# A hand-ordered end of the mixers in a hybrid decoder layer

## The chip, the core and the metric

The kernel runs on one core of a Trainium2 chip. The metric is the device time of one execution in microseconds: 386.02 us is the median of three runs (385.05 to 387.39). TensorE does matmuls, VectorE (DVE) and ScalarE (ACT) elementwise work, GpSimd (POOL) some of it too, and SyncE (SP) issues most DMAs. Each engine runs its own instruction stream in a fixed order; semaphores tie the streams together.

## The reference, cut to what matters

One decoder layer over 256 prompt positions and 8 x 4 decode positions, 288 columns together, model width 1024. The part in which the change lies, in short:

```python
def rmsnorm(x, g):
    y = x * rsqrt(mean(x * x, axis=-1) + 1e-6)
    return y * g

proj = rmsnorm(x) @ w_in                       # -> q | k | v | gate_b | gate_c | u
attn = dilated_attention(rope(q), rope(k), v)  # prompt by itself, decode against its cache
gated_in = gate_c * u
conv = conv_w[0] * u_pad[:, 0:T] + conv_w[1] * u_pad[:, 1:T+1] + conv_w[2] * u_pad[:, 2:T+2]
conv_out = gate_b * conv
mixed = concat(rmsnorm(attn, g_att), rmsnorm(conv_out, g_conv)) @ w_out
x = x + rmsnorm(mixed, n_att_post)
x = x + rmsnorm(square(relu(rmsnorm(x) @ w_up)) @ w_down)
```

## The kernel before

All activations stand transposed: 128 partitions hold features, the 288 columns are positions. Each weight matrix is cut into sub-blocks of 128 x 1024 (s = 0 to 95), which hold the eight 128x128 pieces that yield one chunk of 128 output features; two sub-blocks make one block of 1 MB, and SyncE fetches the blocks in order into three buffers (`raw`). A block's buffer is free for the third block behind it once both its sub-blocks have been split.

A product of 32-bit numbers is made of three matmuls (`mm3`): a weight or an activation is split into a high part, which is a cast by ScalarE, and a low part, which is the difference, taken by VectorE (`split_w`). Then high x high, high x low and low x high are summed in PSUM. So one row (128 input features of one chunk) is three matmuls of 288 columns, and a chunk of eight rows is 24. High and low parts of weights go to buffers of two pools: `splp` (three pairs) and, late in the mixers, `spx` (two pairs).

Sub-blocks 0 to 23 are the input projection. Of them 18 and 20 give the conv gate C of channels 2 and 3 (a channel here is 128 conv features), 19 and 21 give u, and 22 and 23 give the output gate: chunks `B2` and `B3`. Sub-blocks 24 to 31 are the output projection: chunks `mix0` to `mix7`. The first four rows of such a chunk read the normed attention (`mh[0]`, `ml[0]`), the last four the normed conv (`mh[1]`, `ml[1]`). 32 to 63 are the up projection and 64 to 95 the down projection.

At the end of the mixers these steps stand between the products:

- the filter of a channel: one scaling by ScalarE and two taps by VectorE (tile `cv`), then the product with the gate (`conv_out`: a scaling of the PSUM tile to `bs`, and three products into `co`, of 256, 28 and 4 columns);
- the selection of the decode attention: a mask by VectorE (`om`), four small matmuls (`dsel`, the picks, put between rows of B2), and a copy into `aT`;
- the norm of the 32 decode columns (`attd`): a square, a sum over chunks of features, a matmul with a constant matrix that sums over partitions (`ss_attd`), the inverse root by logarithm, exponential and a Newton step (`rsqrt_rows`), the scaling, high and low parts;
- the same for the conv half over all 288 columns (`ss_conv`, `mh1`, `ml1`).

Five projection chunks (`NW = 5`) have their attention half done first, chunk by chunk, while the conv norm is under way; then each of them has its conv half (`mix_half(m, 1, False)`), directly followed by `post` (ScalarE squares the chunk and scales it, VectorE sums the squares). Chunks 5 to 7 are whole products.

The order on each engine is a scheduler's, steered by `tc.high_priority()` and `after(...)` (nothing inside is issued ahead of the named instruction). GpSimd takes the low parts of sub-blocks 24 and 25 (`POOL_LO`) and that of conv chunk 1 (`POOL_ML`). The high and low parts of 25 to 28 are made in four quarters.

Of the kernel before, what the change touches and what calls it, by code (L numbers as in the profile page):

```python
# [10 lines left out]
F32 = mybir.dt.float32  # L11
F32R = mybir.dt.float32r
# [4 lines left out]
P = 128  # L17
# [16 lines left out]
TAIL = ((0, 1, 5), (1, 0, 0), (0, 0, 1), (0, 0, 2), (1, 0, 1), (0, 0, 3), (1, 0, 3), (1, 1, 5), (0, 0, 4), (1, 0, 4),  # L34
        (0, 1, 7), (0, 0, 6), (1, 0, 6), (1, 0, 7))
ORDER = (0, 1, 2, 3, 5, 4, 6, 7)

POOL_LO = (24, 25)
POOL_ML = (1,)

SQ_POOL = 6

# [68 lines left out]
def layer(ctx, tc, xt, vec, cst, kt, vt, st, wts, o_y, o_k, o_v, o_cs):  # L111
# [38 lines left out]
    nc.gpsimd.memset(m512, 1.0 / 512)  # L150


    def split_w(s, parts=1, pool=splp, eng=None):
        raw = blocks[s // 2][:, (s % 2) * 1024:(s % 2) * 1024 + 1024]
        hi = pool.tile([P, 1024], F32R, tag="hi", name=f"hi{s}")
        lo = pool.tile([P, 1024], F32R, tag="lo", name=f"lo{s}")
        n = 1024 // parts
        for i in range(parts):
            cs = slice(i * n, (i + 1) * n)
            a = nc.scalar.copy(hi[:, cs], raw[:, cs])  # L160
            b = (eng or nc.vector).tensor_sub(lo[:, cs], raw[:, cs], hi[:, cs].bitcast(F32))  # L161
# [334 lines left out]
    def d_select(g):  # L496
        om = sm.tile([P, AW], F32, tag="ds", name=f"om{g}", bufs=1)
        nc.vector.scalar_tensor_tensor(
            om.rearrange("p (h d) -> p h d", h=H), dpv[g].rearrange("p (h d) -> p h d", h=H), dpt[g][1],
            c[:, C_DG:C_DG + H].unsqueeze(2).to_broadcast([P, H, HD]), ALU.mult, ALU.mult)  # L500
        ps = pa.tile([P, 512], F32, tag="a", name=f"dsel{g}")

        def pick(p):
            nc.tensor.matmul(ps[:, p * 16:(p + 1) * 16], lhsT=om[:, p * P:(p + 1) * P],
                             rhs=c[:, C_SEL:C_SEL + 16], start=True, stop=True)
            if p == 3:
                nc.vector.tensor_copy(aT[:, :, SEQ + 16 * g:SEQ + 16 * g + 16],
                                      ps[:, 0:64].rearrange("p (c t) -> p c t", c=4))

        return [lambda p=p: pick(p) for p in range(4)]  # L510
# [61 lines left out]
    def group_norm(src, vcol, c0, c1, hf, ssq, nm, pool, tag):  # L572
        n = c1 - c0
        if mh[hf] is None:
            mh[hf] = act.tile([P, 4, NT], F32R, tag="act", name=f"mh{hf}")
            ml[hf] = act.tile([P, 4, NT], F32R, tag="act", name=f"ml{hf}")
        dh, dl = mh[hf], ml[hf]
        s = nrm.tile([P, NT], F32, tag="s", name=f"s_{nm}")
        if n <= 64:
            for ch in range(4):  # L580
                nc.scalar.mul(src[:, ch, c0:c1], src[:, ch, c0:c1], vv[:, vcol + ch:vcol + ch + 1])
        chain = rsqrt_rows(ssq, m512, n, s[:, :n], nm, pool, tag)
        if n <= 64:
            nc.vector.tensor_mul(src[:, :, c0:c1], src[:, :, c0:c1], s[:, :n].unsqueeze(1).to_broadcast([P, 4, n]))
            nc.scalar.copy(dh[:, :, c0:c1], src[:, :, c0:c1])  # L585
            d = nc.vector.tensor_sub(dl[:, :, c0:c1], src[:, :, c0:c1], dh[:, :, c0:c1].bitcast(F32))
            return chain[0], d.ins
        for ch in range(4):
            nc.vector.scalar_tensor_tensor(src[:, ch, c0:c1], src[:, ch, c0:c1], vv[:, vcol + ch:vcol + ch + 1],
                                           s[:, :n], ALU.mult, ALU.mult)  # L590
            nc.scalar.copy(dh[:, ch, c0:c1], src[:, ch, c0:c1])
            e = nc.gpsimd if hf == 1 and ch in POOL_ML else nc.vector
            e.tensor_sub(dl[:, ch, c0:c1], src[:, ch, c0:c1], dh[:, ch, c0:c1].bitcast(F32))
# [53 lines left out]
    es.close()
    pt = ctx.enter_context(tc.tile_pool(name="pt", bufs=6, space=PSUM))
    spx = ctx.enter_context(tc.tile_pool(name="spx", bufs=2, side="right"))
    sqd = cv.tile([P, 4, ND], F32, tag="w", bufs=4, name="sqd")  # L650
    acc_d = cv.tile([P, ND], F32, name="acc_d")
# [7 lines left out]
    b3 = conv_b(3, 23)  # L659
    sq3 = cv.tile([P, NT], F32, tag="w", bufs=4, name="sqc3")  # L660
    with tc.high_priority():
        conv_out(*b3)
        nc.scalar.square(sq3, co[:, 3])
        with after(last_mm[0]):
            group_norm(co, V_CONV, 0, NT, 1, [acc_c, sq3], "conv", pt, "o")
    NW = 5
    ws = [take(24, 0)]
    with after(*chain[:1]):
        ws += [take(25, 0)] + [split_w(26 + m, parts=4, pool=spx) for m in range(2)] + [take(28, 0)]
# [228 lines left out]
```

## Time and profile before

| | |
|---|---|
| median of three runs | 386.02 us (385.05 to 387.39) |
| the profiled execution | 386.36 us, of it 384.6 us span |
| busy in the span | PE 365.8 us (95%), DVE 235.3 (61%), ACT 193.8 (50%), POOL 42.0 (11%) |
| TensorE's granted clock, mean | 0.987 of full speed |
| read from HBM | 73.40 MB, 197 GB/s over the span |
| chain that ended last | PE 79%, DVE 10%, DMA 3%, ACT 3%, issue 2% |

The span is the time from the first to the last instruction; what lies around it counts in the device time too. A share of busy time is a mean over stages with different limits, so a change in one stage is read from the timeline of that stage. In a timeline a row gives the start, the duration and, in brackets, how long the engine stood idle before it and what ended that. Rows of matmuls overlap: a matmul of 288 columns is shown with some 0.30 us, while the next starts 0.13 after it. A fp32 matmul is shown as two instructions. L197 to L199 are the three matmuls of `mm3`.

### The profile page before, as it was taken

What the parts mean: (1) busy time and instruction counts of PE and PEld (TensorE: products, weight loads), DVE (VectorE), ACT (ScalarE), POOL (GpSimd) and SP (SyncE); (2) the same over time, 40 slices, a digit from 0 to 9 for tenths busy, and PEclk for the clock granted to TensorE, in tenths of its full rate; (3) what the DMA queues carried; (4) which work ended last, traced back from release to release, by engine and by line L of the source; (5) the groups of instructions that cost most, each with busy time, mean ns of one, the idle gap of its engine ahead of it and who ended that gap; (6) DMA issues with size and microseconds to landing.
All of it is one profiled execution on the core that took longest, in us unless ns stands there. A gap on an engine that the chain in (4) does not pass through costs nothing.

```text
span 384.6 us, 6800 instructions
## 1 busy us (share of the span) xinstructions
PE 365.8 (95%) x2728; PEld 338.1 (88%) x2728; DVE 235.3 (61%) x424; ACT 193.8 (50%) x370; POOL 42.0 (11%) x69
## 2 busy tenths in 40 slices
PE   7899999999999799999999999999999999999971
PEld 7799777676885699989999999999999999999960
DVE  4998637456484876599886666666434344434416
ACT  5779445534452648537675555555444344434310
POOL 5414100114412500000000000000000000000012
PEclk9999999999999899999999999999999999999996
DMA  6995599996991353801553535353535353542003
GB/s 204 385 402 227 165 416 422 404 356 239 403 418 49 107 201 119 319 3 33 193 211 120 210 114 216 116 211 120 211 118 211 119 210 119 210 125 95 2 0 123
DMA packets 18575, 76.23 MB, mean 198 GB/s; under 512 B 2032, under 2 KB 9200, under 8 KB 11632
## 3 DMA queue, kind: packets, MB, share of 16 engines
q1 hardware_dynamic: 17680, 74.59, 52.5%
q10 hardware_dynamic: 864, 1.22, 0.8%
q8 instruction: 21, 0.34, 0.4%
q14 instruction: 10, 0.08, 0.1%
HBM read 73.40 MB, written 2.40 MB: 197 GB/s over the span
## 4 chain that ended last, share of the span: by engine, by line
PE 79%; DVE 10%; DMA 3%; ACT 3%; issue 2%; SPq 1%; POOL 1%; DVEq 0%; ACTq 0%; POOLq 0%
PE dn L197 9%; PE dn L198 9%; PE dn L199 9%; PE up L197 8%; PE up L199 7%; PE up L198 7%; DMA raw<-wts 3%; PE mix L197 2%; PE mix L198 2%; PE dpv L493 2%; PE mix L199 2%; PE qk L199 2%; PE qk L197 2%; PE qk L198 2%; PE d L449 2%
## 5 line engine op out<-in xcount | busy, mean ns | idle before, releaser
L161 DVE TENSOR_TENSOR lo<-raw,hi 128x1024 fp32r<-128x1024 f32 (+1 forms) x104 | 114.8, 1115 | 81.9 <-ACT hi L160 81.7
L160 ACT CAST hi<-raw 128x1024 fp32r<-128x1024 f32 (+1 forms) x109 | 99.6, 930 | 105.1 <-PE dn L198 56.7
L197 PE MATMUL dn<-fh,hi 128*128 128x288 f32 x256 | 75.8, 296 | 0.0
L198 PE MATMUL dn<-fl,hi 128*128 128x288 f32 x256 | 75.6, 295 | 0.0
L199 PE MATMUL dn<-fh,lo 128*128 128x288 f32 x256 | 75.4, 295 | 0.0
L198 PE MATMUL up<-hl,hi 128*128 128x288 f32 x248 | 73.5, 297 | 0.0
L197 PE MATMUL up<-hh,hi 128*128 128x288 f32 x248 | 73.1, 296 | 0.0
L199 PE MATMUL up<-hh,lo 128*128 128x288 f32 x248 | 73.0, 294 | 0.0
L199 PEld LDWEIGHTS dn<-fh,lo 128*128 128x128 f32 x256 | 48.3, 189 | 0.0
L198 PEld LDWEIGHTS dn<-fl,hi 128*128 128x128 f32 x256 | 48.1, 188 | 0.0
L197 PEld LDWEIGHTS dn<-fh,hi 128*128 128x128 f32 x256 | 48.0, 188 | 0.0
L199 PEld LDWEIGHTS up<-hh,lo 128*128 128x128 f32 x248 | 46.8, 189 | 0.1
L198 PEld LDWEIGHTS up<-hl,hi 128*128 128x128 f32 x248 | 46.6, 188 | 0.1
L197 PEld LDWEIGHTS up<-hh,hi 128*128 128x128 f32 x248 | 46.4, 187 | 0.0
L813 POOL TENSOR_TENSOR mg<-mg,y_f 128x288 f32<-128x288 f32 x1 | 1.0, 1009 | 232.2 <-ACT y_f L209 232.2
L774 DVE SCALAR_TENSOR_TENSOR r<-up,s 128x288 f32<-128x288 f32 x32 | 14.1, 455 | 14.1 <-PE up L199 14.1
L199 PE MATMUL qk<-xh,lo 128*128 128x288 f32 x64 | 18.7, 303 | 2.2 <-DVE lo L250 1.9
L197 PE MATMUL mix<-mh,hi 128*128 128x288 f32 x64 | 19.6, 306 | 1.0 <-ACT mh L585 1.0
L197 PE MATMUL qk<-xh,hi 128*128 128x288 f32 x64 | 19.6, 306 | 0.8 <-ACT hi L249 0.8
L198 PE MATMUL mix<-ml,hi 128*128 128x288 f32 x64 | 19.9, 310 | 0.0
L199 PE MATMUL mix<-mh,lo 128*128 128x288 f32 x64 | 19.5, 305 | 0.0
L198 PE MATMUL qk<-xl,hi 128*128 128x288 f32 x64 | 19.1, 299 | 0.0
(238 smaller groups left out, 628.5 us busy)
## 6 DMA issues: line engine op xcount, KB each, us to landing
raw<-wts SPq DMA_DIRECT2D x45, 1024.0 KB, 4.8
k<-kt SPq DMA_DIRECT2D x16, 640.0 KB, 9.2
v<-vt SPq DMA_DIRECT2D x9, 1024.0 KB, 13.0
raw<-wts SPq DMA_DIRECT2D x4, 512.0 KB, 8.1
o_y<-mg SPq DMA_DIRECT2D x8, 144.0 KB, 1.8
v<-vt SPq DMA_DIRECT2D x2, 512.0 KB, 11.4
x<-xt SPq DMA_DIRECT2D x3, 288.0 KB, 4.4
c<-cst SPq DMA_DIRECT2D x1, 838.0 KB, 9.7
```

Of the source, the lines that this page charges most:

```text
L160: a = nc.scalar.copy(hi[:, cs], raw[:, cs])
L161: b = (eng or nc.vector).tensor_sub(lo[:, cs], raw[:, cs], hi[:, cs].bitcast(F32))
L197: nc.tensor.matmul(ps, lhsT=a, rhs=xh, start=start, stop=False)
L198: nc.tensor.matmul(ps, lhsT=a, rhs=xl, start=False, stop=False)
L199: return nc.tensor.matmul(ps, lhsT=lo[:, j * P:(j + 1) * P], rhs=xh, start=False, stop=stop)
L449: nc.tensor.matmul(ps[32 * i:32 * i + 32, 0:n], lhsT=qbd[:, p, 4 * g + i], rhs=t[:, i, 0:n], start=p == 0, stop=p == 3, tile_position=(0, ...
L493: nc.tensor.matmul(dpv[g][32 * i:32 * i + 32], lhsT=pt[:, j, 32 * i:32 * i + 32], rhs=t[i], start=False, stop=j == 4, tile_position=(0, 32 ...
L774: nc.vector.scalar_tensor_tensor(r, ps[:, :NT], 0.0, s2, ALU.max, ALU.mult)
L813: nc.gpsimd.tensor_mul(mg[:, 0], mg[:, 0], y)
```

## The change

The end of the mixers, from the split of sub-block 23 to the last conv row of projection chunk 4, is put into a block in which the orders of TensorE, VectorE and ScalarE are those of the code. GpSimd has no low parts any more. 26 to 28 are split in whole operations (`high_w`, `low_w`; 28's low part in two halves), 25 too. The splits of 23 and 24 and the filters of channels 2 and 3 stand ahead of the selection, and the picks one row later in B2. The decode columns get their gain by one product on VectorE in place of four on ScalarE. The conv half of chunks 0 to 4 runs row by row: row 0 of all five chunks, then row 1, and so on; the `post` operations follow behind all of it. `prompt_norm` does what `group_norm` did for the prompt.

```diff
-POOL_LO = (24, 25)
-POOL_ML = (1,)
...
-            ready[s] = split_w(s, parts=4 if s in (1, 2) or 25 <= s <= 28 else 1, eng=nc.gpsimd if s in POOL_LO else None)
+            ready[s] = split_w(s, parts=4 if s in (1, 2) else 1)
...
-    picks = d_select(1)
-    b2 = conv_b(2, 22, [lambda: [f() for f in picks[0:2]], lambda: [f() for f in picks[2:4]]])
...
-    with tc.high_priority():
-        nc.scalar.square(sqd, aT[:, :, SEQ:NT])
-        d = nc.vector.tensor_reduce(acc_d, sqd.rearrange("p c t -> p t c"), axis=mybir.AxisListType.X, op=ALU.add)
-        chain = group_norm(aT, V_ATT, SEQ, NT, 0, [acc_d], "attd", pt, "o")
-    with after(chain[0], d.ins):
-        conv_out(*b2)
+    ahead(22)
...
+    with tc.manual_schedule(engines={mybir.EngineType.PE, mybir.EngineType.DVE, mybir.EngineType.Activation}):
+        ahead(23)
+        ahead(24)
+        ys = [conv_y(ch) for ch in (2, 3)]
+        picks = d_select(1)
+        b2 = g_in(22, "B2", [lambda: 0, lambda: [f() for f in picks[0:2]], lambda: [f() for f in picks[2:4]]])
...
+        nc.scalar.square(sqd, ad)
+        nc.vector.tensor_reduce(acc_d, sqd.rearrange("p c t -> p t c"), axis=mybir.AxisListType.X, op=ALU.add)
+        nc.vector.tensor_mul(ad, ad, vv[:, V_ATT:V_ATT + 4].unsqueeze(2).to_broadcast([P, 4, ND]))
+        rsqrt_rows([acc_d], m512, ND, s_d, "attd", pt, "o")
+        nc.vector.tensor_mul(ad, ad, s_d.unsqueeze(1).to_broadcast([P, 4, ND]))
+        nc.scalar.copy(mh[0][:, :, SEQ:NT], ad)
+        conv_out(2, b2, ys[0])
+        nc.vector.tensor_sub(ml[0][:, :, SEQ:NT], ad, mh[0][:, :, SEQ:NT].bitcast(F32))
         sq_add(acc_c, co[:, 2], "sqc2", False)
+        ahead(25)
+        b3 = g_in(23, "B3")
+        ws = [take(24, 0), take(25, 0)] + [high_w(26 + i, spx) for i in range(2)]
+        conv_out(3, b3, ys[1])
...
+        ws.append(high_w(28, splp))
+        low_w(26, ws[2])
+        low_w(27, ws[3])
+        low_w(28, ws[4], 0, 512)
...
+        mix_rows(0, 0, range(4))
+        mix_rows(1, 0, range(2))
+        s_c = nrm.tile([P, NT], F32, tag="s", name="s_conv")
+        rsqrt_rows([acc_c, sq3], m512, NT, s_c, "conv", pt, "o")
...
+        conv_norm(0)
+        low_w(28, ws[4], 512)
+        for ch in range(4):
+            nc.vector.tensor_sub(ml[1][:, ch], co[:, ch], mh[1][:, ch].bitcast(F32))
+            if ch < 3:
+                conv_norm(ch + 1)
+        mix_rows(1, 0, range(2, 4))
+        for m in range(2, NW):
+            mix_rows(m, 0, range(4))
+        for j in range(4):
+            for m in range(NW):
+                mix_rows(m, 1, [j])
...
     for m in range(8):
         if m < NW:
-            mix_half(m, 1, False)
             ps = pss[m]
```

VectorE around the selection of the second decode group, before (`uu3` is the last input of the filters, `lo23` the low part of sub-block 23, `cv3` the taps of channel 3, `om1` the mask, `dsel1` what the picks give):

```order
L537 TENSOR_TENSOR uu3_1521<-u3_1496,s0_157 128x288
L546 SCALAR_TENSOR_TENSOR cv3_1636<-gt_685,vv_78,cv3_1636 128x304 x2
L498 SCALAR_TENSOR_TENSOR om1_1554<-dpv1_1525,rd1_1421,c_177 128x512
L161 TENSOR_TENSOR lo23_1562<-raw11_255,hi23_1561 128x1024
L507 COPY aT_182<-dsel1_1556 128x4x16
L654 TENSOR_REDUCE acc_d_1608<-sqd_1607 128x32
L552 TENSOR_TENSOR bs2_1628<-B2_1565,s0_157 128x288
```

And after the change:

```order
L545 TENSOR_TENSOR uu3_1523<-u3_1498,s0_157 128x288
L158 TENSOR_TENSOR lo23_1559<-raw11_255,hi23_1558 128x1024
L158 TENSOR_TENSOR lo24_1563<-raw12_264,hi24_1562 128x1024
L554 SCALAR_TENSOR_TENSOR cv2_1566<-gt_685,vv_78,cv2_1566 128x304 x2
L554 SCALAR_TENSOR_TENSOR cv3_1570<-gt_685,vv_78,cv3_1570 128x304 x2
L506 SCALAR_TENSOR_TENSOR om1_1574<-dpv1_1527,rd1_1421,c_177 128x512
L515 COPY aT_182<-dsel1_1576 128x4x16
L668 TENSOR_REDUCE acc_d_1620<-sqd_1619 128x32
```

The mask stood behind one filter's taps and ahead of `lo23`; now it stands behind `lo23`, `lo24` and the taps of both channels.

ScalarE behind the conv half of the projection, before (`hi29` and `hi30` are the high parts for chunks 5 and 6; `q_m`, `ssm`, `mg` and `gm` are the post operations of the chunk named at the right):

```order
L160 CAST hi29_1908<-raw14_268 128x1024
L699 ACTIVATE ssm_1823<-mix0_1741 128x288
L700 ACTIVATE mg_1820<-mix0_1741,vv_78 128x288
L721 ACTIVATE gm_1824<-mix0_1741,vpp_1826 128x288
L699 ACTIVATE q_m1_1856<-mix1_1754 128x288
L700 ACTIVATE mg_1820<-mix1_1754,vv_78 128x288
L160 CAST hi30_1912<-raw15_270 128x1024
L699 ACTIVATE q_m2_1872<-mix2_1767 128x288
L700 ACTIVATE mg_1820<-mix2_1767,vv_78 128x288
```

And after the change, from the first post operation on (`hi29` stands right ahead of it):

```order
L729 ACTIVATE ssm_1860<-mix0_1693 128x288
L730 ACTIVATE mg_1857<-mix0_1693,vv_78 128x288
L750 ACTIVATE gm_1861<-mix0_1693,vpp_1863 128x288
L729 ACTIVATE q_m1_1869<-mix1_1694 128x288
L730 ACTIVATE mg_1857<-mix1_1694,vv_78 128x288
L729 ACTIVATE q_m2_1873<-mix2_1695 128x288
L730 ACTIVATE mg_1857<-mix2_1695,vv_78 128x288
L729 ACTIVATE q_m3_1877<-mix3_1696 128x288
L730 ACTIVATE mg_1857<-mix3_1696,vv_78 128x288
L729 ACTIVATE q_m4_1881<-mix4_1697 128x288
L730 ACTIVATE mg_1857<-mix4_1697,vv_78 128x288
L157 CAST hi30_1889<-raw15_270 128x1024
```

`hi30` stood behind the post operations of chunks 0 and 1; now it stands behind those of all five chunks.

## Rows read from the trace of the kernel before

**Rows 1.** Stretches of the span: busy us (instructions) by engine, PEclk, DMA share, GB/s.

```profile
132.00:136.00 4.00, 3.99 (x17) 3.77 (x17) 4.00 (x13) 2.78 (x10) 0.58 (x1) 0.57 0.57 188
136.00:160.00 24.00, 24.00 (x181) 23.83 (x179) 16.75 (x28) 16.43 (x33) 0.91 (x1) 1.00 0.55 192
```

**Rows 2.** Timeline of TensorE, 109 to 160 us: start, us, engine, line, operation, tiles.

```profile
109.71 0.65 PE L475 MATMUL dt<-ident,ds 128*128 128x128 f32 x4
...
120.85 0.40 PE L197 MATMUL B<-xh,hi 128*128 128x288 f32 x1
...
122.15 0.52 PE L504 MATMUL dsel<-c,om 128*128 128x16 f32 x4
...
128.43 0.29 PE L199 MATMUL B<-xh,lo 128*128 128x288 f32 x1
...
131.64 0.40 PE L197 MATMUL mix<-mh,hi 128*128 128x288 f32 x1 [1.01 <-ACT mh L585]
...
135.91 0.30 PE L199 MATMUL mix<-mh,lo 128*128 128x288 f32 x1
...
159.64 0.65 PE L205 MATMUL ss_mix<-ssm,m 128*128 128x288 f32 x2
```

**Rows 3.** The chain that ended last, 125 to 132 us: start, us, what.

```profile
126.58 2.28 DVE co L557
...
128.88 0.45 ACT sqc L569
...
129.36 0.46 DVE acc_c L570
129.82 0.67 DVE s_attd L214
...
130.50 0.76 DVE aT L584
```

**Rows 4.** Timeline of VectorE, 104 to 165 us.

```profile
118.32 1.11 DVE L546 SCALAR_TENSOR_TENSOR cv<-gt,vv,cv 128x304 f32<-128x304 f32 x2 [1.80 <-ACT cv L544]
120.99 0.75 DVE L498 SCALAR_TENSOR_TENSOR om<-dpv,rd,c 128x512 f32<-128x512 f32 x1 [1.57 <-PE dpv L493]
...
125.56 0.46 DVE L552 TENSOR_TENSOR bs<-B,s 128x288 f32<-128x288 f32 x1 [1.04 <-PE B L199]
...
133.22 0.15 DVE L557 TENSOR_TENSOR co<-bs,cv 128x4 f32<-128x4 f32 x1
...
144.79 1.23 DVE L161 TENSOR_TENSOR lo<-raw,hi 128x1024 fp32r<-128x1024 f32 x1 [1.71 <-ACT hi L160]
```

**Rows 5.** Timeline of GpSimd, 104 to 165 us.

```profile
126.39 2.44 POOL L161 TENSOR_TENSOR lo<-raw,hi 128x1024 fp32r<-128x1024 f32 x1 [8.42 <-ACT hi L160]
```

**Rows 6.** Timeline of ScalarE, 104 to 165 us.

```profile
107.93 0.55 ACT L544 ACTIVATE cv<-gt,vv 128x304 f32<-128x304 f32 x1 [4.54 <-POOL gt L539]
...
118.00 0.34 ACTq L684 DMA_DIRECT2D o_cs<-cst_t  x1
118.44 1.05 ACT L160 CAST hi<-raw 128x1024 fp32r<-128x1024 f32 x1 [0.15 <-issue]
123.80 0.31 ACT L653 ACTIVATE sqd<-aT 128x128 f32<-128x128 f32 x1 [4.31 <-DVE aT L507]
...
143.71 1.05 ACT L160 CAST hi<-raw 128x1024 fp32r<-128x1024 f32 x1 [0.36 <-PE mix L198]
144.66 0.41 ACT L699 ACTIVATE ssm<-mix 128x288 f32<-128x288 f32 x1
...
145.73 0.42 ACT L699 ACTIVATE q_m<-mix 128x288 f32<-128x288 f32 x1
...
146.40 1.07 ACT L160 CAST hi<-raw 128x1024 fp32r<-128x1024 f32 x1
```

**Rows 7.** DMA issues of the whole span: count, KB each, median us to landing.

```profile
raw<-wts SPq DMA_DIRECT2D x45, 1024.0 KB, 4.8
```

**Rows 8.** Timeline of TensorE, 9 to 14 us.

```profile
11.98 0.40 PE L199 MATMUL qk<-xh,lo 128*128 128x288 f32 x1 [1.11 <-DVE lo L250]
```

More of the change, by code (lines that the diff above doesn't have):

```diff
@@ L150, in layer, with split_w @@
     nc.gpsimd.memset(m512, 1.0 / 512)
-    def split_w(s, parts=1, pool=splp, eng=None):
+    def split_w(s, parts=1, pool=splp):
         raw = blocks[s // 2][:, (s % 2) * 1024:(s % 2) * 1024 + 1024]
@@ L160, in split_w @@
             a = nc.scalar.copy(hi[:, cs], raw[:, cs])
-            b = (eng or nc.vector).tensor_sub(lo[:, cs], raw[:, cs], hi[:, cs].bitcast(F32))
+            b = nc.vector.tensor_sub(lo[:, cs], raw[:, cs], hi[:, cs].bitcast(F32))
         splits[s] = a.ins, b.ins
@@ L165, in layer, with raw_of, high_w, low_w @@
     splits = {}
+    def raw_of(s):
+        return blocks[s // 2][:, (s % 2) * 1024:(s % 2) * 1024 + 1024]
+    def high_w(s, pool):
+        w = [pool.tile([P, 1024], F32R, tag=n, name=f"{n}{s}") for n in ("hi", "lo")]
+        nc.scalar.copy(w[0], raw_of(s))
+        return w
+    def low_w(s, w, a=0, z=1024):
+        nc.vector.tensor_sub(w[1][:, a:z], raw_of(s)[:, a:z], w[0][:, a:z].bitcast(F32))
     def after(*ins):
@@ L539, in conv_u, with conv_y @@
         nc.gpsimd.tensor_mul(b6(gt[:, ch, 258:306])[:, :, 2:6], b6(cc[ch][:, SEQ:NT]), b6(uu[:, SEQ:NT]))
-    def conv_b(ch, s, between=()):
+    def conv_y(ch):
         w3 = [vv[:, V_TAP + 4 * t + ch:V_TAP + 4 * t + ch + 1] for t in range(3)]
@@ L546, in conv_b @@
             nc.vector.scalar_tensor_tensor(y, gt[:, ch, t:t + 304], w3[t], y, ALU.mult, ALU.add)
+        return y
+    def conv_b(ch, s, between=()):
+        y = conv_y(ch)
         return ch, g_in(s, f"B{ch}", between), y
@@ L570, in sq_add, with prompt_norm @@
             (e or nc.vector).tensor_add(acc, acc, t[:, :n])
[L572 to L587, printed above, removed]
-        for ch in range(4):
[L589 to L593, printed above, removed]
+    def prompt_norm():
+        for i in range(2):
+            mh[i] = act.tile([P, 4, NT], F32R, tag="act", name=f"mh{i}")
+            ml[i] = act.tile([P, 4, NT], F32R, tag="act", name=f"ml{i}")
+        s = nrm.tile([P, NT], F32, tag="s", name="s_attp")
+        rsqrt_rows([acc_a[:, 0:SEQ]], m512, SEQ, s[:, :SEQ], "attp", pa, "a")
+        for ch in range(4):
+            a, h = aT[:, ch, 0:SEQ], mh[0][:, ch, 0:SEQ]
+            nc.vector.scalar_tensor_tensor(a, a, vv[:, V_ATT + ch:V_ATT + ch + 1], s[:, :SEQ], ALU.mult, ALU.mult)
+            nc.scalar.copy(h, a)
+            nc.vector.tensor_sub(ml[0][:, ch, 0:SEQ], a, h.bitcast(F32))
     v_chunk(0)
@@ L635, in layer @@
     acc_c = cv.tile([P, NT], F32, tag="acc", name="acc_c")
-    group_norm(aT, V_ATT, 0, SEQ, 0, [acc_a[:, 0:SEQ]], "attp", pa, "a")
+    prompt_norm()
     conv_c(3, 20)
@@ L644, in layer @@
         sq_add(acc_c, co[:, ch], f"sqc{ch}", ch == 0, nc.gpsimd)
-    picks = d_select(1)
-    b2 = conv_b(2, 22, [lambda: [f() for f in picks[0:2]], lambda: [f() for f in picks[2:4]]])
[L647 to L651, printed above, removed]
-    with tc.high_priority():
-        nc.scalar.square(sqd, aT[:, :, SEQ:NT])
-        d = nc.vector.tensor_reduce(acc_d, sqd.rearrange("p c t -> p t c"), axis=mybir.AxisListType.X, op=ALU.add)
-        chain = group_norm(aT, V_ATT, SEQ, NT, 0, [acc_d], "attd", pt, "o")
@@ L656, in layer @@
-    with after(chain[0], d.ins):
-        conv_out(*b2)
-        sq_add(acc_c, co[:, 2], "sqc2", False)
[L659 to L662, printed above, removed]
-        nc.scalar.square(sq3, co[:, 3])
[L664 to L669, printed above, removed]
@@ L670, in layer, with mix_rows, conv_norm @@
-    pss = []
-    def mix_half(m, hf, start):
-        if start:
-            pss.append((pg if m < 2 else pt).tile([P, 512], F32, tag="g" if m < 2 else "o", name=f"mix{m}"))
+    ahead(22)
+    NW = 5
+    pss = []
+    def mix_rows(m, hf, js):
+        for j in js:
+            mm3(pss[m][:, :NT], ws[m], 4 * hf + j, mh[hf][:, j], ml[hf][:, j], hf == 0 and j == 0, hf == 1 and j == 3)
+    with tc.manual_schedule(engines={mybir.EngineType.PE, mybir.EngineType.DVE, mybir.EngineType.Activation}):
[4 more added lines that the diff above has]
+        b2 = g_in(22, "B2", [lambda: 0, lambda: [f() for f in picks[0:2]], lambda: [f() for f in picks[2:4]]])
+        es.close()
+        pt = ctx.enter_context(tc.tile_pool(name="pt", bufs=6, space=PSUM))
+        spx = ctx.enter_context(tc.tile_pool(name="spx", bufs=2, side="right"))
+        sqd = cv.tile([P, 4, ND], F32, tag="w", bufs=4, name="sqd")
+        acc_d = cv.tile([P, ND], F32, name="acc_d")
+        ad = aT[:, :, SEQ:NT]
+        s_d = nrm.tile([P, NT], F32, tag="s", name="s_attd")[:, :ND]
+        nc.scalar.square(sqd, ad)
[6 more added lines that the diff above has]
+        nc.vector.tensor_sub(ml[0][:, :, SEQ:NT], ad, mh[0][:, :, SEQ:NT].bitcast(F32))
+        sq_add(acc_c, co[:, 2], "sqc2", False)
+        ahead(25)
+        b3 = g_in(23, "B3")
+        ws = [take(24, 0), take(25, 0)] + [high_w(26 + i, spx) for i in range(2)]
+        conv_out(3, b3, ys[1])
+        sq3 = cv.tile([P, NT], F32, tag="w", bufs=4, name="sqc3")
+        nc.scalar.square(sq3, co[:, 3])
+        ws.append(high_w(28, splp))
[3 more added lines that the diff above has]
+        for m in range(NW):
+            pss.append((pg if m < 2 else pt).tile([P, 512], F32, tag="g" if m < 2 else "o", name=f"mix{m}"))
+        mix_rows(0, 0, range(4))
+        mix_rows(1, 0, range(2))
+        s_c = nrm.tile([P, NT], F32, tag="s", name="s_conv")
+        rsqrt_rows([acc_c, sq3], m512, NT, s_c, "conv", pt, "o")
+        def conv_norm(ch):
+            a, h = co[:, ch], mh[1][:, ch]
+            nc.vector.scalar_tensor_tensor(a, a, vv[:, V_CONV + ch:V_CONV + ch + 1], s_c, ALU.mult, ALU.mult)
+            nc.scalar.copy(h, a)
+        conv_norm(0)
[7 more added lines that the diff above has]
+            mix_rows(m, 0, range(4))
@@ L675, in mix_half @@
         for j in range(4):
-            mm3(pss[m][:, :NT], ws[m], 4 * hf + j, mh[hf][:, j], ml[hf][:, j], start and j == 0, not start and j == 3)
-    for m in range(NW):
-        mix_half(m, 0, True)
+            for m in range(NW):
+                mix_rows(m, 1, [j])
     cst_t = cv.tile([P, 4, 18], F32, name="cst_t")
```

## The prediction, as it was put on record

> **What bounds the kernel now.** I read three views: the busy shares by stretch, the timeline of TensorE in the stretch that the change rewrites, and the chain of waits through it. From 136 to 160 us TensorE runs 181 instructions in 24.00 us at clock 1.00 [rows 1]: one matmul of 288 columns takes 0.133 us, a chunk of 24 takes 3.2 us, and nothing is to be had there but by taking matmuls away, which the change does not do. The loss lies just before. [...] From 128.56, when TensorE could have gone on, to 135.91, TensorE does 14 projection matmuls and two of the sum of squares ss_conv (about 0.5 at full speed): 14 x 0.133 + 0.5 = 2.4 us of work in 7.35. So about 4.95 is lost: 2.85 in waits (the 3.1 up to 131.64 less one half of ss_conv), the rest, 2.1, in slow matmuls, of which some 0.35 is restarts and the low clock about 1.75. The chain says what ends last there [rows 3]: a product on 128x4 elements that takes 2.28 us, then a square, a sum and the scale of the decode rows, all on VectorE and ScalarE. The same product is over in 0.15 at 133.22 [rows 4]; between them only one thing differs that a row shows: GpSimd ran a low part from 126.39 to 128.83 [rows 5].
>
> **The change, part by part.** My sum starts from the profiled execution (386.36 us, span 384.6, so 1.8 outside the span); the median shown is 386.02, 0.34 less, and I carry the difference over to it.
>
> Low parts off GpSimd. Three go to VectorE: two of 1.23 (as at 144.79, [rows 4]) and one of 0.46 (a 288-wide operation, as at 125.56). VectorE is busy 16.75 of 24 in the late stretch [rows 1], so the room is there; what they cost is their place, below. The 2.28 us product becomes 0.15: 2.1 off the chain. [...]
>
> Filters moved. Before, ScalarE's filter start for channel 2 stands ahead of the softmax of the last decode group and waits for GpSimd until 107.93 [rows 6]. With it gone, that chain starts about 0.2 earlier, and with it the transposes at 109.71 [rows 2], for which TensorE pauses 0.25: -0.2, between 0 and -0.25.
>
> Splits and filters ahead of the selection. This is the first new wait. ScalarE's order is now: store of the conv state (118.00, 0.34), high parts of 23 and 24, both filter starts [rows 6]. VectorE's is lo23, lo24, four filter taps, and only then om, the selection's mask; before, om stood right behind two taps and began when its matmuls ended, 120.99 [rows 4]. Worked out, 0.2 earlier all through: the store at 117.8, hi23 118.24 to 119.29, hi24 to 120.23 (0.95 apart, as 143.71 and 144.66), lo23 119.32 to 120.55, lo24 to 121.69, four taps at 0.55 (two take 1.11) to 123.73, om 123.65 to 124.40. TensorE gets to the first two selection matmuls earlier: before they issued at 122.15 [rows 2]; one row of three matmuls more stands ahead of them and all is 0.2 earlier, so 122.15 + 0.4 - 0.2 = 122.35, and about 122.45 with the step between two kinds of matmul. They wait until 124.45: +2.0. Bounds: if hi23 came 1 us earlier, 1.0; if GpSimd's copies ahead of the store came later by as much, 3.0. I take 2.0, since all terms but the 0.2 are rows. Behind the waiting selection matmuls on TensorE stands the rest of B2 and all of B3, and what waits for them is the decode norm. [...]
>
> Decode norm. One multiplication by the gain on VectorE (about 0.3) in place of four on ScalarE, its sum of squares after B2's last row. It lies beside B3. B3's end moves with the selection wait, by -0.2 + 2.0 + 0.1 for the restart, from 128.56 to 130.45; the low part is done at about 130.3. Cost 0; if it slips by 0.5, 0.35.
>
> Then VectorE is late again. The second pair of picks issues 0.85 behind the first, 125.3, and is through at 125.8; copy, square, reduce, the sum behind B2's last row (127.0), logarithm, exponential, three small steps and the scale (0.2 to 0.4 each) bring VectorE to 129.0; B2's scaling and product take it to 130.0, square and sum (0.45 and 0.46, [rows 3]) to 131.0; hi25 stands on ScalarE behind that square, 130.4 to 131.45; lo25 to 132.7; B3's scaling (0.46, [rows 4]) to 133.1. Projection chunk 1 takes B3's PSUM buffer, so its first matmul waits for that scaling. Chunk 0's 12 matmuls run 130.45 to 132.05: it waits from 132.05 to 133.1: +1.05, between 0.5 and 1.6, plus 0.1 for the restart. The bounds are half a us either way, for small steps of which not each has its row.
>
> Quarters made whole, low parts of 26 to 28. Whole operations cost less than four quarters; lo26 is done at 134.9 and needed at 135.4, the others later. Cost 0; cover 0.5 us. The conv norm starts at 136.5 on VectorE, and a row costs about 1.4 (scale, cast, low part at 0.45 each); TensorE has 42 matmuls behind ss_conv until 140.2. Row by row over five chunks it takes 2.0 a row. Slack about 0.6 at the first row, growing. Cost 0.
>
> The five chunks now end almost together. The first chunk's weights are let go 15 - 3 matmuls before the end of the conv half, not 6.4 us before chunk 5. ScalarE's hi29 begins 0.33 after the last matmul on it has issued, as now (143.71, [rows 6]): 146.7 to 147.75; lo29 to 149.0, needed at 148.5: +0.55. Then come all post operations of five chunks on ScalarE before hi30: first chunk 1.07, four at 0.67 (144.66 to 145.73 and 145.73 to 146.40, [rows 6]), 3.75 in all: hi30 from 151.4 to 152.45, lo30 to 153.75. Chunk 6 is due at 152.1, its third matmul at 152.35: +1.4. Before, hi30 stood ahead of chunk 2's post. Bounds for the two together 1.2 and 2.6. With 0.2 for two restarts. Chunk 7's and the next stage's splits follow in time (lo31 at 155.3, due 156.8).
>
> Loads: weight block 17 (sub-blocks 34, 35) is asked for when lo29 is done, 149.0 for 146.05; with 4.8 to landing [rows 7] it is there before hi34's turn on ScalarE at 155. Cost 0; without that cover 1.
>
> Sum: -0.2 + 2.0 + 0.1 - 4.95 + 1.15 + 0.55 + 1.4 + 0.2 and 0.1 for the step behind ss_conv = +0.35. The same walk ends the projection at 160.0, against 159.64 now [rows 2]. 386.02 + 0.35 is 386.4. Behind that the chain (norm, up and down projections) is the same.
>
> **Rivals.** A, faster: the waits shrink. For it: the old gap and low clock, 4.95, surely sit in this stretch, and my new waits are worked out from an order, with small steps that can run closer. Against: om behind the taps and hi30 behind ten post operations are fixed orders. With the selection wait at its lower bound 1.0, the two late ones at 1.2 and the one of chunk 1 at 0.5, it is 2.3 less: 384.1; with no wait at all 381.2.
>
> B, slower: the clock falls again. Its place is the selection wait in B2 (2.0 us in one piece) or chunks 5 and 6. For it: the clock of 0.57 after B3 came behind two waits with only ss_conv between. Against: at the start TensorE waits 1.11 and goes on at full speed [rows 8], and the old pause was 3.1 long with little in it. Price: the 1.75 of before where TensorE is the bound (chunks 5 to 7), 388.1; about 0.7 in B3, since chunk 1's wait takes up 1.05 of it: 387.1. It decides from a wait of more than about 2.5 us.
>
> C: the long product isn't due to GpSimd. Then its 2.1 stays on VectorE ahead of lo25 and lengthens chunk 1's wait: 388.5.
>
> **How the numbers follow.** Forecast 0.60, 386.4, with 384.8 to 387.9 as its own range (1.5 each way from the bounds above). A 0.18, B 0.18, C 0.04. About 0.5% (1.9 us) is what a measurement of this kernel tells from no change. The forecast leaves 0.02 on the fast side and 0.03 on the slow one, A gives 0.16 to faster, B and C together 0.20 to slower and 0.02 to no change: faster 0.18, no change 0.59, slower 0.23. The range 384.0 to 388.7 holds most of A and B and leaves out the best case of A and a clock that falls twice.
>
> **What would show it.** GpSimd without low parts, the 128x4 product at about 0.15. TensorE waiting for om before the first selection matmuls in B2, about 2 us; a wait of about 1 at the start of projection chunk 1, for B3's scaling; no wait in the conv half; waits of about 0.5 and 1.4 at lo29 and lo30. The gap of 3.1 behind B3 gone, and 132 to 136 at clock 1.00. I am wrong if the selection matmuls don't wait, if hi30 comes early, or if the clock is low after 124.

## The result, and the profile after

The changed kernel takes 389.0 us (median of 6 runs, 388.7 to 390.25) where the kernel before took 385.12 beside it: a ratio of 1.0088, interval 1.0066 to 1.011. Measured a second time it was 388.25 against 386.03, ratio 1.0060 [1.0041, 1.0079]. So it is slower, by 0.6 to 0.9%, where I forecast no change at 386.4. The first measurement lies just above the range of 384.0 to 388.7, the second inside it. The profiled execution took 388.7 us, 386.9 of it span, against 386.36 and 384.6 before.

First the stretches: the last two answer to [rows 1], the two ahead of them are new (length, then busy us of TensorE, its weight loads, VectorE, ScalarE, GpSimd, then granted clock, DMA share, GB/s):

```profile
124.00:128.00 4.00, 3.37 (x19) 3.37 (x20) 1.37 (x4) 0.31 (x1) 0.00 (x0) 0.72 0.20 84
128.00:132.00 4.00, 4.00 (x28) 4.00 (x28) 2.03 (x9) 1.27 (x5) 0.00 (x0) 0.85 0.00 0
132.00:136.00 4.00, 3.25 (x23) 2.99 (x22) 3.46 (x7) 3.60 (x5) 0.00 (x0) 1.00 0.21 39
136.00:160.00 24.00, 22.52 (x163) 21.67 (x163) 16.19 (x28) 15.16 (x30) 0.00 (x0) 1.00 0.41 147
```

The low clock has not gone, it has moved: from 132 to 136 to the two stretches before. And from 136 on TensorE is no longer full (22.52 of 24.00). Its timeline, answering [rows 2] (start, us, engine, line, operation, tiles; in brackets the idle time before and what ended it):

```profile
122.42 0.30 PE L207 MATMUL B<-xh,lo 128*128 128x288 f32 x1
124.63 0.62 PE L512 MATMUL dsel<-c,om 128*128 128x16 f32 x4 [1.91 <-DVE om L506]
...
127.44 0.44 PE L207 MATMUL B<-xh,lo 128*128 128x288 f32 x1
127.68 0.44 PE L205 MATMUL B<-xh,hi 128*128 128x288 f32 x1
...
128.40 0.47 PE L213 MATMUL ss_attd<-acc_d,m 128*128 128x32 f32 x2
...
132.07 0.29 PE L207 MATMUL B<-xh,lo 128*128 128x288 f32 x1
132.20 0.29 PE L205 MATMUL mix<-mh,hi 128*128 128x288 f32 x1
...
133.67 0.29 PE L207 MATMUL mix<-mh,lo 128*128 128x288 f32 x1
134.71 0.37 PE L205 MATMUL mix<-mh,hi 128*128 128x288 f32 x1 [0.75 <-DVE bs L564]
...
150.97 0.40 PE L207 MATMUL mix<-mh,lo 128*128 128x288 f32 x1 [0.40 <-DVE lo L158]
154.50 0.40 PE L205 MATMUL mix<-mh,hi 128*128 128x288 f32 x1 [0.34 <-ACT hi L157]
155.76 0.40 PE L207 MATMUL mix<-mh,lo 128*128 128x288 f32 x1 [0.73 <-DVE lo L158]
161.99 0.65 PE L213 MATMUL ss_mix<-ssm,m 128*128 128x288 f32 x2
```

Read it from the top. TensorE waits for the mask om ahead of the selection matmuls. Some matmuls later the issues stand 0.24 apart (127.44, 127.68), no longer 0.133; the granted clock is 0.72 in that stretch. B3 then runs into chunk 0 without a gap (132.07, 132.20; before, 128.43 and 131.64), so the old loss is gone. Chunk 1 waits for the scaling of B3, and chunks 5 and 6 for their splits. The statistic ss_mix ends the stretch at 161.99, against 159.64 before: 2.35 later, which is the difference of the two spans (2.3). What follows takes 224.9 to 225.0 us in both.

On VectorE, against [rows 4], the products are short and the mask late:

```profile
121.79 2.12 DVE L554 SCALAR_TENSOR_TENSOR cv<-gt,vv,cv 128x304 f32<-128x304 f32 x4
123.83 0.75 DVE L506 SCALAR_TENSOR_TENSOR om<-dpv,rd,c 128x512 f32<-128x512 f32 x1
...
129.54 0.19 DVE L218 SCALAR_TENSOR_TENSOR t_attd<-y_attd 128x32 f32<-128x32 f32 x1 [2.08 <-ACT y_attd L217]
...
131.35 0.16 DVE L569 TENSOR_TENSOR co<-bs,cv 128x4 f32<-128x4 f32 x1
...
134.11 0.45 DVE L564 TENSOR_TENSOR bs<-B,s 128x288 f32<-128x288 f32 x1
```

ScalarE, against [rows 6], has all post operations ahead of the high part of chunk 6:

```profile
148.61 1.05 ACT L157 CAST hi<-raw 128x1024 fp32r<-128x1024 f32 x1 [2.93 <-PE mix L206]
149.56 0.40 ACT L729 ACTIVATE ssm<-mix 128x288 f32<-128x288 f32 x1
...
153.32 1.13 ACT L157 CAST hi<-raw 128x1024 fp32r<-128x1024 f32 x1
```

GpSimd runs nothing from 120 to 160 us. The 128x4 product takes 0.16 where it took 2.28 [rows 3]. In the middle VectorE is idle for 2.08 us, waiting for the logarithm and exponential behind ss_attd: the place that matters below.

### The profile page after: what moved, and what is told of

Same layout as the page of the kernel before. It is cut to its first block, busy times and chain, and to the rows that moved or that the text cites. A ratio compares the mean times of both kernels' runs of the same rounds, so it can differ in the third digit from the quotient of the medians.

```text
span 386.9 us, 6783 instructions
## 1 busy us (share of the span) xinstructions
PE 365.9 (95%) x2728; PEld 338.4 (87%) x2728; DVE 233.2 (60%) x420; ACT 191.6 (50%) x354; POOL 35.7 (9%) x63
## 4 chain that ended last, share of the span: by engine, by line
PE 56%; DVE 8%; ACT 3%; issue 2%; POOL 0%; ACTq 0%; DVEq 0%; POOLq 0%
PE dn L205 9%; PE dn L207 9%; PE dn L206 9%; PE up L205 7%; PE up L206 7%; PE up L207 7%; PE mix L205 2%; PE mix L207 2%; PE mix L206 2%; DVE lo L158 1%; ACT hi L157 1%; DVE mg L853 1%; DVE mg L760 1%; DVE x L761 1%; DVE hl L776 1%
## 5 line engine op out<-in xcount | busy, mean ns | idle before, releaser
L158 DVE TENSOR_TENSOR lo<-raw,hi 128x1024 fp32r<-128x1024 f32 (+1 forms) x94 | 112.4, 1205 | 84.8 <-ACT hi L157 84.7
L157 ACT CAST hi<-raw 128x1024 fp32r<-128x1024 f32 (+1 forms) x94 | 95.1, 1025 | 109.6 <-PE dn L206 56.7
L206 PE MATMUL mix<-ml,hi 128*128 128x288 f32 x64 | 18.9, 295 | 0.0
```

What stands on the lines that cost most here:

```text
L158: b = nc.vector.tensor_sub(lo[:, cs], raw[:, cs], hi[:, cs].bitcast(F32))
L206: nc.tensor.matmul(ps, lhsT=a, rhs=xl, start=False, stop=False)
```

## The experiments

Times are medians; a ratio is to the kernel before on the same chip. All edits are to the changed kernel unless said otherwise. My reading of the trace is this: the loss is the selection wait, the low clock behind it and the late splits. In each text of what was expected, theory 1 is what this reading says of that run, and the others are rivals.

**The mask first.** One line moves ahead of lo24 and the four filter taps.

```diff
         ahead(23)
+        picks = d_select(1)
         ahead(24)
         ys = [conv_y(ch) for ch in (2, 3)]
-        picks = d_select(1)
```

> The changed kernel, with the selection's mask om moved on VectorE from behind lo24 and the four filter taps to right behind lo23; nothing else. Theory 1 (the new wait and the low clock that it brings are most of the loss): the first selection matmuls no longer wait (under 0.3 us for 1.91), the granted clock stays 1.00 from 124 to 130 us, chunk B3 ends about 3 us earlier, and most of that is kept: about 3.0 less than the changed kernel, 386.0 us. Theory 2 (VectorE is simply late with all the work that GpSimd gave up, wherever the order puts it): what the selection gains is lost again at the start of projection chunk 1, whose wait grows from 0.75 to over 2; at most 0.7 less, 388.3 us or more.

386.53 us, ratio 1.0011 [0.9994, 1.0028]. TensorE's timeline:

```profile
122.94 0.51 PE L512 MATMUL dsel<-c,om 128*128 128x16 f32 x4
...
126.33 0.38 PE L213 MATMUL ss_attd<-acc_d,m 128*128 128x32 f32 x2 [0.75 <-DVE acc_d L668]
...
132.55 0.37 PE L205 MATMUL mix<-mh,hi 128*128 128x288 f32 x1 [0.96 <-DVE bs L564]
```

The selection no longer waits, the granted clock is 1.00 all through from 108 to 164, and the loss against before is gone. One line of order is worth 0.77% against the first measurement of the changed kernel (1.0088 to 1.0011) and 0.49% against the second (1.0060): 2 to 3 us. What is left is VectorE's chain, for which ss_attd now waits 0.75 and chunk 1 still 0.96, and the waits of chunks 5 and 6, unchanged (0.40, 0.34 and 0.73).

**High part of chunk 6 early.**

```diff
+    ahead(29)
+    ahead(30)
     for m in range(8):
         if m < NW:
```

> The changed kernel, with the high and low parts of sub-blocks 29 and 30 asked for ahead of the post operations, so that on ScalarE hi30 stands right behind hi29; nothing else. Theory 1 (the wait of chunk 6 is made by hi30 standing behind ten post operations): no wait at chunk 6 (0.34 + 0.73 before, with 0.2 for restarts), that of chunk 5 (0.40) stays, about 1.2 less: 387.8 us. Theory 2 (ScalarE and VectorE are full there, and something else is then late): a wait of about 1 at chunk 7 for hi31 or lo31, or at the norm behind the projection; at most 0.3 less.

387.08 us, ratio 1.0039 [1.0021, 1.0057], 0.7 below theory 1. The chunk 6 wait is gone, as forecast: it came from hi30's place behind the ten post operations. The wait of chunk 5, which I expected to stay, has gone too, and hi30's place on ScalarE doesn't explain that: chunks 5 to 7 stand outside the hand-ordered block, and with hi30 asked for early the scheduler changed TensorE's order as well. It puts the first two matmuls of chunk 6, which need hi30, ahead of chunk 5's first with a low part (TensorE, then ScalarE):

```profile
149.84 0.29 PE L206 MATMUL mix<-ml,hi 128*128 128x288 f32 x1
150.22 0.40 PE L205 MATMUL mix<-mh,hi 128*128 128x288 f32 x1
...
150.59 0.35 PE L207 MATMUL mix<-mh,lo 128*128 128x288 f32 x1
...
148.17 1.99 ACT L157 CAST hi<-raw 128x1024 fp32r<-128x1024 f32 x2 [2.93 <-PE mix L206]
```

The second of these rows starts when hi30 is done (150.16), the third when lo29 is. So this run changes two orders at once. The selection wait is as it was (1.91), the clock falls again:

```profile
124.00:128.00 4.00, 3.30 (x21) 3.30 (x22) 1.45 (x4) 0.31 (x1) 0.00 (x0) 0.80 0.23 94
128.00:132.00 4.00, 4.00 (x26) 4.00 (x26) 2.44 (x10) 1.70 (x5) 0.00 (x0) 0.77 0.00 0
```

In this execution the fall is a little smaller: chunk 1 starts at 134.27, 0.44 earlier than in the changed kernel's profile, and ss_mix at 159.99, 2.00 earlier. So 1.56 of the 2.00 is due to the edit.

**Matmuls in the wait.** Eight matmuls on a constant fill the selection wait; nothing reads what they write.

```diff
-        b2 = g_in(22, "B2", [lambda: 0, lambda: [f() for f in picks[0:2]], ...
+        b2 = g_in(22, "B2", [lambda: 0, lambda: [filler()] + [f() for f in picks[0:2]], ...
```

> The changed kernel, with eight matmuls of a constant tile (128 columns, nothing reads them) put on TensorE ahead of the first selection matmuls, to fill the wait there. Theory 1 (the low clock after the wait costs time of its own): the selection matmuls start at the same time, within 0.3 us, the granted clock stays 1.00 in 124 to 130, chunk B2's sum of squares and all behind it is about 1.5 us earlier: 387.5 us. Theory 2 (the low clock is hidden, since VectorE's chain to projection chunk 1 is the bound): the clock is 1.00 too, but chunk 1 starts where it started, 134.7: at most 0.3 less, 388.7 us.

388.03 us, ratio 1.0063 [1.0043, 1.0083], half a us above what theory 1 said. That is 1.0 less than the first measurement of the changed kernel (389.0, ratio 1.0088), but only 0.2 less than the second (388.25, ratio 1.0060).

```profile
122.57 1.95 PE L663 MATMUL fill<-m 128*128 128x128 f32 x16
124.65 0.62 PE L512 MATMUL dsel<-c,om 128*128 128x16 f32 x4
...
127.29 0.38 PE L213 MATMUL ss_attd<-acc_d,m 128*128 128x32 f32 x2
...
133.51 0.38 PE L205 MATMUL mix<-mh,hi 128*128 128x288 f32 x1 [0.96 <-DVE bs L564]
```

This is the test of the clock in the trace. The selection starts where it did (124.65 against 124.63), the clock is 1.00 from 124 to 132, and then ss_attd is 1.1 earlier, chunk 1 and ss_mix 1.2 earlier (160.79 for 161.99). So the low clock of that execution costs 1.2, and it comes through in full up to ss_mix. The times don't show this gain: the interval overlaps both of the changed kernel's.

**GpSimd alone.** The kernel *before*, with POOL_LO and POOL_ML empty and nothing else changed.

> The kernel before, with the three low parts of GpSimd (sub-blocks 24 and 25, conv chunk 1) on VectorE and the order left to the scheduler; this is one part of the change alone. Theory 1 (GpSimd's low part held up the 128x4 product): that product takes about 0.15 us for 2.35, and the wait behind chunk B3 gets shorter by 0.5 to 1.5, since lo24 and lo25 now stand on VectorE ahead of the decode norm: 383.8 to 384.8 us against 385.1. Theory 2 (the product is long by itself, or the work that moves to VectorE costs as much as the hold-up): the product stays above 2, or the time is 385.1 to 386.5.

384.27 us, ratio 0.9962 [0.9948, 0.9977]: the change's first part alone makes the kernel faster, as theory 1 said. The 128x4 product takes 0.15; ss_mix stands at 157.13 (159.64 before, in an execution with the low clock; the medians differ by 1.4). Not all of the old gap goes (VectorE, then TensorE):

```profile
126.55 0.15 DVE L557 TENSOR_TENSOR co<-bs,cv 128x4 f32<-128x4 f32 x1
...
130.95 0.75 PE L205 MATMUL ss_conv<-sqc,m 128*128 128x288 f32 x2 [1.69 <-ACT sqc L663]
131.32 0.65 PE L197 MATMUL mix<-mh,hi 128*128 128x288 f32 x2
```

In the scheduler's order ss_conv stands ahead of chunk 0 and waits for a square. The hand order has it behind the first two rows of chunk 1; no run tests that move alone.

**Both edits.** The mask first and hi30 early together.

> The changed kernel with both edits of the first experiments: the mask written ahead of the second low part, and the high part of chunk 6 cast ahead of the ten post operations. Theory 1 (the selection wait with the low clock behind it, and the late split of chunk 6, are two separate losses): they add. From 386.5 with the first edit alone, the waits 0.40, 0.34 and 0.73 of chunks 5 and 6 go, so 384.9 (384.4 to 385.5); no wait of TensorE in chunks 5 and 6, ss_mix near 158.4. Theory 2 (one of them hides the other, and VectorE's chain sets the end either way): 386.0 or more, with a new wait of over 1 us between chunk 1 and the statistic ss_mix.

384.9 us, ratio 0.9974 [0.9955, 0.9992]. They add: 1.0011 and 1.0039 against 1.0088 make 0.9962, against 1.0060 they make 0.9990, and both lie in the interval. No wait is left behind chunk 1; ss_mix is at 157.78. With its two misplaced lines mended the hand order is thus no faster than the part without GpSimd alone (0.9962); the gain over that part begins with the next two edits.

**Taps of channel 3 later.** Beside both edits, they move behind the gain of the decode columns.

```diff
         nc.vector.tensor_mul(ad, ad, vv[:, V_ATT:V_ATT + 4]...)
+        conv_taps(3, y3, w3)
         rsqrt_rows([acc_d], m512, ND, s_d, "attd", pt, "o")
```

> The kernel with both edits, and in it the two filter taps of channel 3 written behind the scaling of the selection's rows, no longer ahead of the copy of the selection. Theory 1 (on VectorE the taps stand in the way of the copy, and with it of the statistic ss_attd and of all that follows to chunk 1): ss_attd starts without its wait of 0.75, the scaling bs of channel 3 comes 0.8 earlier, chunk 1 too, and the time falls by 0.8 below the kernel with both edits (0.5 to 1.1). Theory 2 (chunk 1 waits for something that the taps don't move, the low part 25 or the bank itself): the wait at ss_attd becomes a wait of the same size at chunk 1, within 0.3 of the kernel with both edits.

383.77 us, ratio 0.9944 [0.9918, 0.997], 1.1 less, in intervals that overlap; in the traces ss_mix is 0.80 earlier (156.98). The wait at ss_attd is gone, chunk 1 starts 0.78 earlier (131.26 against 132.04) and waits 0.96 as before: VectorE's whole chain moved, up to chunk 1.

**Low part 25 out of the way of B3's scaling.** Beside the late taps:

```diff
+        w25 = high_w(25, splp)
         nc.scalar.copy(mh[0][:, :, SEQ:NT], ad)
...
+        low_w(25, w25)
         sq_add(acc_c, co[:, 2], "sqc2", False)
-        ahead(25)
```

> The kernel with the late taps, and in it the high part 25 cast ahead of the decode rows' high part on ScalarE, and the low part 25 ahead of the sum of squares on VectorE, so that the scaling bs of channel 3 no longer stands behind a low part that waits for its cast. Theory 1 (VectorE's chain to bs of channel 3 sets the start of chunk 1): the idle 0.31 and 0.48 of VectorE ahead of that low part go, chunk 1's wait shrinks from some 0.9 to 0.3, and the time falls by 0.5 (0.2 to 0.8) below the kernel with the late taps. Theory 2 (what chunk 1 no longer waits for is waited for later, at the rows of the conv half or in the weights of chunks 5 to 7): no change within 0.3, with a wait of TensorE of 0.5 or more behind chunk 1 that the kernel with the late taps has not.

383.15 us, ratio 0.9922 [0.9897, 0.9946]: the lowest time of all, and faster than both kernels. The 0.6 against the late taps alone is within the two intervals; in the traces it is 33.39 us from the selection to ss_mix, for 34.46 there. TensorE's timeline has no row with a wait of note left from B2 to ss_mix:

```profile
130.75 0.29 PE L207 MATMUL mix<-mh,lo 128*128 128x288 f32 x1
130.93 0.40 PE L205 MATMUL mix<-mh,hi 128*128 128x288 f32 x1
...
156.64 0.65 PE L213 MATMUL ss_mix<-ssm,m 128*128 128x288 f32 x2
```

**Conv half chunk by chunk.** With the mask first, row by row is undone.

```diff
-        for j in range(4):
-            for m in range(NW):
-                mix_rows(m, 1, [j])
+        for m in range(NW):
+            mix_rows(m, 1, range(4))
```

> The kernel with the mask first, and in it the conv half chunk by chunk, as in the kernel before: all four rows of chunk 0, then of chunk 1, and so on. Theory 1 (row by row hides the conv norm's rows, and puts off the posts and with them the splits of chunks 5 and 6): TensorE waits within chunk 0 for the low parts of rows 1 to 3, 1.2 in all (rows ready at 140.2, 141.6 and 143.0 against a need from 140.2 on), and no longer in chunks 5 and 6, where 1.47 go, so 386.3, 0.2 below the kernel with the mask first (0.6 below to 0.3 above). Theory 2 (the waits of chunks 5 and 6 come from the order on ScalarE alone and stay): 387.7. Theory 3 (the conv norm's rows are ready in time in either order): 385.1.

385.87 us, ratio 1.0000 [0.9984, 1.0016], against 1.0011 with the mask first alone: no difference that can be measured. The trace agrees with theory 1. The waits of chunks 5 and 6 are gone, new ones stand in chunk 0:

```profile
140.89 0.40 PE L205 MATMUL mix<-mh,hi 128*128 128x288 f32 x1 [0.16 <-ACT mh L696]
142.27 0.40 PE L205 MATMUL mix<-mh,hi 128*128 128x288 f32 x1 [0.36 <-ACT mh L696]
```

The idle time in brackets is 0.52. By the issues it is more, since the matmuls behind these two wait as well: the seven steps from 140.43 to 143.13 take 2.70 for 0.93, so 1.8 is lost, some 0.2 of it in restarts (0.40 for 0.29 at each), where I expected 1.2. From the selection to ss_mix it is 36.42 us (122.70 to 159.12), against 36.89 with the mask first (122.94 to 159.83). So row by row as written gives back late what it saves early; with hi30 early it need not (35.34 with both edits).

**The changed kernel again.**

> The changed kernel once more, unedited, beside the next kernel and the kernel before on one chip, to see how well the result stands. Theory 1 (the loss is in its order, at the selection wait with the low clock and at the late splits of chunks 5 and 6): 3.4 above before again (2.6 to 4.3), the granted clock below 0.9 between 124 and 132, the selection's wait at 1.9. Theory 2 (the first measurement caught before low or the clock's fall was chance): less than 2 above before, or no fall of the clock in the profile.

388.25 us, ratio 1.0060 [1.0041, 1.0079]: 2.2 above before, between the two theories' bounds (2.6 and 2.0). The wait is 1.91 again, and this execution (389.6 us) has the fall longer (two stretches, then TensorE):

```profile
124.00:128.00 4.00, 3.24 (x15) 3.25 (x16) 1.15 (x4) 0.31 (x1) 0.00 (x0) 0.63 0.23 98
128.00:132.00 4.00, 4.00 (x19) 4.00 (x18) 1.78 (x8) 0.82 (x3) 0.00 (x0) 0.52 0.00 0
...
129.29 0.47 PE L213 MATMUL ss_attd<-acc_d,m 128*128 128x32 f32 x2
...
135.60 0.37 PE L205 MATMUL mix<-mh,hi 128*128 128x288 f32 x1
```

So the loss stands, its size varies, and the fall with it. From ss_attd to chunk 1 it is 6.31 us here, 6.31 in the first profile and 6.22 with the filler, though here TensorE stays slow up to 131.87 and chunk 1 has no wait left. So slow rows behind ss_attd are covered; what costs time are those between the selection and ss_attd (4.53 us here, 3.77 in the first profile, 2.64 with the filler).

**Low part 25 on GpSimd.** The best version, with `low_w(25, w25, e=nc.gpsimd)`.

> The kernel with the early low part 25, and in it that low part on GpSimd, as the kernel before had it; all else stays. Theory 1 (while GpSimd works on a low part, an instruction of VectorE does not end): GpSimd works on it from about 127.8 to 130.3, one of VectorE's products for channel 2 takes some 2 us instead of 0.4 or less and ends with it, the decode rows' low part follows it, TensorE waits 1.2 at the second matmul of chunk 0 and some 0.3 at chunk 1, and the time is 1.4 above the kernel with the early low part (0.9 to 2.7, the upper end with a fall of the clock), though VectorE has 1.2 less to do. Theory 2 (the two engines work side by side): no product is longer than 0.5, and the time is that of the kernel with the early low part or up to 0.4 below.

384.44 us, ratio 0.9964 [0.9943, 0.9986], 1.3 above the best version's 383.15, as theory 1 said (1.4); ss_mix comes 1.44 later (158.08). GpSimd's timeline first:

```profile
127.80 2.38 POOL L173 TENSOR_TENSOR lo<-raw,hi 128x1024 fp32r<-128x1024 f32 x1 [9.15 <-ACT hi L169]
```

and VectorE's of the same run:

```profile
127.70 0.45 DVE L569 TENSOR_TENSOR bs<-B,s 128x288 f32<-128x288 f32 x1
128.18 2.27 DVE L570 TENSOR_TENSOR co<-bs,cv 128x256 f32<-128x256 f32 x1
130.38 0.17 DVE L572 TENSOR_TENSOR co<-bs,cv 128x28 f32<-128x28 f32 x1
```

This time the 128x256 product is the long one (2.27, otherwise 0.43); it ends 0.27 behind the low part. The scaling bs, which starts 0.10 ahead of GpSimd's row, takes its usual 0.45. TensorE waits 1.34 in chunk 0 for the decode rows' low part.

## Why the prediction was wrong

Most steps held. One was mis-priced, and it makes 1.2 of the 2.0 us by which the trace misses my sum.

- *Low parts off GpSimd, 2.28 to 0.15.* Right: 0.16 after, 0.15 with that part alone, and 2.27 again on another product once a low part is put back. Rival C is out. Why the product is held, no run shows.
- *The old gap, −4.95.* The gap went, as forecast. But 1.75 of it was the low clock of one execution (0.57 in [rows 1], behind the last matmul of B3 at 128.43, [rows 2]), and the spread of the times suggests that before does not have it each time (below).
- *Filters moved, −0.2.* Came, and is hidden: the transposes start at 109.71 in both profiles, but this execution reached the stretch 0.17 later (ss_attp at 107.63, before 107.46). The pause ahead of the transposes shrank as forecast, from 0.25 to 0.08. With the later start the mask was 0.2 later than forecast. Before, then after:

```profile
109.33 0.29 PE L198 MATMUL C<-xl,hi 128*128 128x288 f32 x1
109.71 0.65 PE L475 MATMUL dt<-ident,ds 128*128 128x128 f32 x4
...
109.50 0.29 PE L206 MATMUL C<-xl,hi 128*128 128x288 f32 x1
109.71 0.66 PE L483 MATMUL dt<-ident,ds 128*128 128x128 f32 x4
```

- *Selection wait, 2.0.* Right. From the issue at 122.42 TensorE could have gone on at 122.55; it went on at 124.63, 2.1 later. VectorE kept its written order: om starts at 123.83, behind the four taps (2.12 from 121.79). ScalarE kept its own: the filter starts at 120.34 stand behind the high parts of 23 and 24 (1.99 from 118.44). With one moved line the selection starts at 122.94 without a wait.
- *Chunk 1 (1.05), chunks 5 and 6 (0.55 and 1.4).* Right in place and size. By the issues: 133.80 to 134.71 is 0.91, though both ends came 1.6 to 1.8 later than forecast, so that the size of this wait is partly luck; chunk 5 lost 0.56 (150.41 to 150.97), chunk 6 about 1.4. No wait came in the conv half, as forecast.
- *The failed step: the low clock behind the selection wait, which the sum puts at nothing, and rival B's price and condition for it.* I named the place, the selection wait in B2, and the mechanism, the clock falling again. Then I set the price there to "about 0.7 in B3, since chunk 1's wait takes up 1.05 of it", and the condition to a wait "of more than about 2.5 us", an estimate between the 1.11 [rows 8] and the 3.1 of before. Both are wrong. The clock fell in this profile behind 2.1 us without a matmul (0.72 from 124 to 128). And for the rows ahead of ss_attd there was no cover: chunk 1's wait ends with B3's scaling on VectorE, and that scaling stands behind the decode norm, which waits for ss_attd, a matmul behind B2's slow rows. I had treated the VectorE chain as fixed while TensorE slowed down. In truth both sides moved together: ss_attd was forecast at 127.0 and came at 128.40, VectorE's idle 2.08 is that wait, chunk 1 was forecast at 133.1 and came at 134.71. The filler run gives 1.2 of this to the clock. For the rows behind ss_attd the cover did hold, as the second profile of the changed kernel shows. A low clock after 124 was among my own signs of being wrong.
- *The rest of the sum.* Chunk 1 was 1.6 late (0.2 of it the later start of the stretch, 1.2 the clock, 0.2 small steps). The two matmuls of ss_conv with the step behind them took 0.98 (135.57 to about 136.55) for my 0.6: 0.4 more. That makes the 2.0 between forecast (160.0) and measured (161.99).
- *From the trace to the times.* The trace difference is 2.3 us, the times differ by 3.9 and 2.2. The profiled execution of before (386.36) lies 1.2 above the median that was measured beside the first (385.12), so the trace starts from one of its slower executions.

Two rivals of these experiments fell as well: one loss does not hide another (both edits add), and VectorE's chain is not an end that nothing can move (two reorderings on it shortened the way from the selection to ss_mix by 0.9 and 1.1).

Open: why the clock falls in some executions of one program and not in others, and whether the changed kernel has executions without it. Those with a mean clock of 0.987 or more in the second measurement (387.68 to 388.46) suggest a smaller fall, and so do the four of twelve with hi30 early, which keeps the selection wait, that have 0.990 (385.85 to 387.01; the other eight 386.77 to 388.72), but they were not profiled.

## What to carry to other kernels

When an order is written by hand, look for the one instruction that TensorE waits for and write it ahead of all bulk work on its engine; here a mask of 0.75 us behind lo24 and four taps cost 2 to 3 us. A wait counts as cover for a slow stretch only if what ends it doesn't itself hang on that stretch: follow the chain back from the waiting instruction before booking the cover. Test the parts of such a change one by one, since its good part (384.27 alone) was hidden here by two misplaced lines. And where a scheduler sets the orders, look at every engine's order after an edit: hi30 early was meant for ScalarE and VectorE and changed TensorE's too.

## What the runs showed of the hardware that was not expected

- The granted clock is not the same in each execution of a program. Over the 74 executions of the kernel before that ran beside the experiments, 32 had a mean clock of 0.990 or more and a median of 385.3 us, 42 had less and a median of 386.5. That fits a fall like that of [rows 1] in some and not in others; that it is the same stretch was not seen.
- Pauses of TensorE in the profiles: 1.34 (low part 25 on GpSimd) and 1.69 (before without GpSimd) were followed by a clock of 1.00; 1.91 was followed by a fall in all three profiles that have it (0.72, 0.80 and 0.63 from 124 to 128); the same stretch with 1.95 us of filler matmuls in it was not (1.00).
- While GpSimd made a low part in one piece (2.44 us before, 2.38 in the last run), one VectorE product that starts shortly behind it was held in each of these profiles: the 128x4 one before (2.28, without it 0.15), the 128x256 one in the last run (2.27, otherwise 0.43). Not each one was held: before, the 128x28 product, which starts 0.01 behind GpSimd's row, took its usual 0.18. While GpSimd made low part 25 in quarters, two more were long: the scale of the decode rows and its product took 0.67 and 0.76 before [rows 3], and 0.19 and 0.29 in the changed kernel.
